# Two conditioning slices summed on VectorE, a later division, and another ring for the odd layer's conditioning tiles

## Chip, cores and metric

The kernel runs on one core of one Trainium2 chip. The metric is the device time of one execution in microseconds; lower is better. PE is TensorE, DVE VectorE, ACT ScalarE, POOL GpSimd, SP SyncE, whose queue issues most transfers.

## The reference

A two-layer diffusion backbone over 512 latent tokens (a grid of 8 rows and 64 columns, 1024 channels) and 256 context tokens. Cut to what matters here:

```python
for l in range(2):
    sh1, sc1, g1, sh2, sc2, g2 = split(silu(c) @ ada_w[l] + ada_b[l], 6)   # ada_w: (1024, 6144) per layer
    u = rmsnorm(x, norm1_g[l]) * (1 + sc1) + sh1
    y = even_mixer(u, u_ctx) if l == 0 else odd_mixer(u)
    x = x + g1 * (y @ w_out[l])
    x = x + g2 * hier_moe(rmsnorm(x, norm2_g[l]) * (1 + sc2) + sh2)

# even_mixer: q, k, v and three convolution inputs by projection; 8 heads of neighbourhood attention over
# 512 window keys and the context keys together: softmax(q k / 8 + bias) v, beside a short gated convolution
# odd_mixer: three Hyena parts (long convolutions by a DFT) beside a Conformer convolution; 20 projections
```

The 6144 conditioning columns of a layer are three slices of 2048: slice (l, 0) is sh1 and sc1, (l, 1) is g1 and sh2, (l, 2) is sc2 and g2. Only sh1 and sc1 of layer 0 are needed at the start; the others are due later.

## The kernel before

All is fp32. A large product is done as three matmuls of rounded parts (`mm3`, lines 159 to 161): `split` (lines 145 and 146) makes `whi` on ACT and `wlo` on DVE from a loaded 512 KB tile `raw`. The tiles come from rings: `raw` has 5 buffers, `whi` and `wlo` 4 each. A ring gives its oldest buffer, so a load waits on the SP queue until the last reader of that buffer is done, and everything behind it on SP waits too.

The program runs in stages: the start of the conditioning and the K projection (to about 76 us), V, Q and the twelve gated-convolution projections `proj_ch` (to about 210), the attention (to about 310), `w_out`, routing and sixteen expert blocks of layer 0 (to about 590), the odd layer with twenty projections `P(c)`, four long convolutions (`chain`) and four Conformer parts (to about 835), then `w_out` and experts again.

The conditioning slices are spread as a filler through two stages. `ada` (line 209) loads two 512 KB tiles per step and multiplies them on PE with the column `cT` (line 225; 32 output columns, four column groups side by side; 64 records per slice). `ada_sums` (line 229) adds the tiles on DVE instead, scaled by the conditioning value (lines 246 and 248), and sums over the partitions by four matmuls (line 254). Before the change `rest` (line 449) runs slices (0,1), (0,2) and (1,0) by `ada`; the odd layer runs (1,1) and (1,2) by `ada_sums`. `tick` advances the filler by `PRE[0]` per V and Q tile, `PRE[1]` per `proj_ch` and `PRE[2]` per attention step. The first slice's tiles go into the four attention-bias buffers (`self.spare`), which are free until the attention bias is loaded; the later ones into the `raw` ring. In the odd layer `ORDER` mixes the steps (`t1`) with projections, and the sums' tiles share the `raw` ring with `w_in_odd` (20 tiles) and `cfx` (4).

The attention has 16 steps (4 pairs of heads, 4 query tiles). `scores` (line 540) adds the bias and takes the row maximum on DVE (line 554), the exponential and its sum `z` on ACT (line 558). `values` (line 562) divides the probabilities by `z` on DVE (lines 565 and 566), transposes them on PE (line 569), copies them (lines 572 and 574) and multiplies by V (line 580). After four steps `ya` is split (lines 604 and 605).

Each engine runs its instructions in one fixed order. A scheduler sets it when the kernel is built, so a change in one place can move instructions elsewhere. At line 225 one step does:

```python
for g in range(4):
    nc.tensor.matmul(ps[32 * g:32 * g + 32, :], self.cT[:, k, :],
                     raws[g // 2][:, (g % 2) * 512:(g % 2) * 512 + 512], start=(k == 0), stop=(k == 7))
```

Of the kernel before, what the change touches and what calls it, by code (L numbers as in the profile page):

```python
# [8 lines left out]
F32 = mybir.dt.float32  # L9
# [3 lines left out]
AF = mybir.ActivationFunctionType  # L13
ALU = mybir.AluOpType
# [5 lines left out]
LN_EPS = 1e-5  # L20
WIN0 = (0, 64, 192, 256)
PAT = (0, 1, 1, 2)
PRE = [0.4, 0.5, 1.5]
PLO = (0, 0)
HMD = [[1, 2, 3], [0, 1, 3]]
HMA = [[], [0, 1, 2]]
# [35 lines left out]
PM = 1  # L62
PJ = 2
PU = [[], []]
ORDER = 'p1 t1 v1 t1 v0 t1 p0 t1 c0 t1 A0 t1 v3 t1 v2 t1 p2 t1 c2 t1 p3 t1 c1 t1 A1 x0 t1 c3 t1 x1 t1 B0 t1 x2 L0 x3 B1 t9'
TWO_PI = (6.28125, 0.0019350051879882812, float(2.0 * math.pi - 6.28125 - 0.0019350051879882812))
P_, Q_ = (0, 1, 2, 3), (4, 5, 6, 7)
NP1, NP2, NQ2, NQ3 = 8, 9, 10, 11
# [2 lines left out]
class Build:  # L71
# [158 lines left out]
    def ada_sums(self, l, j):  # L230

        nc, A = self.nc, self.A
        b = A["ada_b"]
        bias = self.wk.tile([128, 512], F32, tag="t2", name="adab")
        nc.gpsimd.dma_start(bias, bass.AP(tensor=b.tensor, offset=b.offset + l * 6144 + j * 2048,
                                          ap=[[512, 4], [0, 32], [1, 512]]))
        for h in range(2):
            acc = self.ep2.tile([128, 1024], F32, tag="adaacc", name="adaacc", bufs=1)
            c0 = j * 2048 + h * 1024
            for k in range(8):  # L240
                raw = self.spare.pop(0) if self.spare else self.rawp.tile([128, 1024], F32, tag="raw", name="raw")
                if self.spare:
                    self.spare.append(raw)
                nc.sync.dma_start(raw, A["ada_w"][l, k * 128:k * 128 + 128, c0:c0 + 1024])
                if k == 0:
                    nc.vector.tensor_scalar(acc, raw, self.cT[:, k, 0:1], None, op0=ALU.mult)
                else:
                    nc.vector.scalar_tensor_tensor(acc, raw, self.cT[:, k, 0:1], acc, op0=ALU.mult, op1=ALU.add)
                if k % 2:
                    yield  # L250
            if not h:
                ps = self.mmt()
            for g in (2 * h, 2 * h + 1):
                nc.tensor.matmul(ps[32 * g:32 * g + 32, :], self.onec.to_broadcast([128, 32]), acc[:, (g % 2) * 512:(g % 2) * 512 + 512],
                                 start=True, stop=True)
        self.ada_done(l, j, ps, bias)

    def ada_done(self, l, j, ps, bias):
        nc, A = self.nc, self.A
# [117 lines left out]
    def even(self, st):  # L377
        nc, A = self.nc, self.A
# [3 lines left out]
        ep2 = self.ep2 = self.pool(st, "ep2", 2)  # L382
# [11 lines left out]
        bias = [ep.tile([128, 4, 256], F32, name=f"bias{i}") for i in range(4)]  # L394
# [53 lines left out]

        def rest():
            for l, j in ((0, 1), (0, 2), (1, 0)):  # L450
                yield from self.ada(l, j)

        self.fill, self.due, self.hold = rest(), 0, None
        W = WV
# [52 lines left out]
        for s in range(4):  # L507
# [6 lines left out]
            m = ep2.tile([128, 528], F32, tag="cm", name="cm", bufs=1)  # L514
# [19 lines left out]
            if s == 2:  # L534
                qk = prep(0)
# [1 line left out]
        vblk = ((vt[:, 0, :], vt[:, 1, :]), (vs[:, 0, :], vs[:, 1, :]), (vs[:, 1, :], vs[:, 2, :]),  # L537
                (vt[:, 2, :], vt[:, 3, :]))

        def scores(qk, j):  # L540

            qs, ks, bs = qk
            pes = []
            for i in range(2):
                s = self.sct()
                for n0, k0 in ((0, WIN0[j]), (256, 512)):
                    for p in range(2):
                        nc.tensor.matmul(s[:, n0:n0 + 256], qs[:, i, p, j * 128:j * 128 + 128],
                                         ks[:, i, k0:k0 + 256], start=(p == 0), stop=(p == 1))
                pt = PAT[j]  # L550
                bsl = bs[i][:, pt:4:3 - pt, :]
                pe = ep2.tile([128, 512], F32, tag="pe", name="pe", bufs=4)
                nm = ep2.tile([128, 1], F32, tag="nm", name="nm", bufs=4)
                nc.vector.tensor_tensor_reduce(pe.rearrange("p (a b) -> p a b", a=2),
                                               s.rearrange("p (a b) -> p a b", a=2), bsl, -1.0, 3.0e38,
                                               op0=ALU.add, op1=ALU.min, accum_out=nm)
                z = ep2.tile([128, 1], F32, tag="z", name="z", bufs=4)
                nc.scalar.activation(pe, pe, AF.Exp, bias=nm, scale=-1.0, accum_out=z)
                pes.append((pe, z))
            return pes  # L560

        def values(c, j, pes, pv):
            pts = []
            for i, (pe, z) in enumerate(pes):
                nc.vector.reciprocal(z, z)
                nc.vector.tensor_scalar(pe, pe, z, None, op0=ALU.mult)
                tp = self.trt()
                for bl in range(4):
                    nc.tensor.transpose(tp[:, bl * 128:bl * 128 + 128], pe[:, bl * 128:bl * 128 + 128], self.ident)  # L569
                pT = ep2.tile([128, 4, 128], F32, tag="pT", name="pT", bufs=3)  # L570
                if i == 0:
                    nc.scalar.copy(pT.rearrange("p a b -> p (a b)"), tp)
                else:
                    nc.vector.tensor_copy(pT.rearrange("p a b -> p (a b)"), tp)
                pts.append(pT)
            for bl in range(4):
                for i in range(2):
                    h = 2 * c + i
                    v = vblk[j][bl] if bl < 2 else vt[:, 2 + bl, :]
                    nc.tensor.matmul(pv[64 * i:64 * i + 64, j * 128:j * 128 + 128], v[:, h * 64:h * 64 + 64],  # L580
                                     pts[i][:, bl, :], start=(bl == 0), stop=(bl == 3))

        ya = [self.bp.tile([128, 4, 512], F32R, tag="b8", name="ya") for _ in range(2)]
        pes = scores(qk, 0)
        for n in range(16):
            c, j = n // 4, n % 4
            if j == 0:
                pv = self.mmt()
            if j == PJ and c < 3:
                qk2 = prep(c + 1)  # L590
            if j == 3 and c < 3:
                qk = qk2
                if c < 2:
                    rel_bias(c + 2)
            nxt = scores(qk, (j + 1) % 4) if n < 15 else None
            self.tick(PRE[2])
            if n == 13:
                for _ in self.fill:
                    pass
                self.W0 = self.chunk(A["w_out"][0], 0)  # L600
            values(c, j, pes, pv)
            pes = nxt
            if j == 3:
                nc.scalar.copy(ya[0][:, c, :], pv)
                nc.vector.tensor_tensor(ya[1][:, c, :], pv, ya[0][:, c, :], op=ALU.subtract)
        self.yh = [ya[0][:, s, :] for s in range(4)] + [yc[0][:, s, :] for s in range(4)]
        self.yl = [ya[1][:, s, :] for s in range(4)] + [yc[1][:, s, :] for s in range(4)]

# [204 lines left out]
    def odd(self, st):  # L813
# [80 lines left out]
        fill = self.ada1  # L894
        for w in ORDER.split():
            if w[0] == "t":
# [631 lines left out]
```

## Time and profile before

| | |
|---|---|
| median of 3 runs | 1126.87 us (1123.34 to 1130.07) |
| the profiled execution | 1123.78 us |
| its span, first to last instruction | 1121.7 us, so 2.1 us lie around it |
| mean granted TensorE clock | 0.944 |
| busy share of the span | PE 91%, DVE 69%, ACT 44%, POOL 21% |

The profile gives busy time per engine, the chain of work that ended last, groups of instructions, and by stretch the granted TensorE clock and the share of the DMA engines. Matmuls overlap: a matmul's duration is longer than the step from one start to the next, so a stretch is read by start times.

### The profile page before, as it was taken

The page shows a single profiled execution, that of the slowest core. Times are in us where ns is not written, and L with a number is a line of the kernel's source. Part 1 is how long each engine was busy: PE and PEld are TensorE (multiplying, and loading weights), DVE is VectorE, ACT ScalarE, POOL GpSimd, SP SyncE. Part 2 cuts the span into 40 slices and gives each one's busy share as a digit, 9 for nine tenths or more (in the row PEclk, how much of TensorE's full clock was granted, in tenths as well). Part 3 has the DMA queues.
Part 4 walks back from the last instruction along what each step waited for, and adds up shares of the span by engine and source line. Part 5 has one row for each costly group of instructions (what it writes and reads, how often), then busy time and mean ns, then how long its engine had stood idle before and what let it go on. Part 6 is the DMA issues. An engine that isn't in the chain of part 4 may idle for free.

```text
span 1121.7 us, 14655 instructions
## 1 busy us (share of the span) xinstructions
PE 1023.0 (91%) x5118; PEld 755.2 (67%) x5118; DVE 774.0 (69%) x1255; ACT 497.9 (44%) x787; POOL 230.4 (21%) x244
## 2 busy tenths in 40 slices
PE   6999999999999599999987889899899859999994
PEld 2786787556787477777756667576477747777663
DVE  3462335587658798897967677757754577998883
ACT  3352223356434476577625323221253236766652
POOL 2031304011053223354221000000002121333311
PEclk8999999998999599999988899899989778999998
DMA  8825563686364479999825657634418786799893
GB/s 342 319 68 166 164 198 128 245 267 220 121 222 177 153 228 349 307 317 299 270 61 205 224 148 232 192 94 142 140 56 268 258 269 211 242 307 322 283 291 79
DMA packets 75374, 240.78 MB, mean 215 GB/s; under 512 B 15887, under 2 KB 17706, under 8 KB 75296
## 3 DMA queue, kind: packets, MB, share of 16 engines
q1 hardware_dynamic: 59840, 209.82, 55.0%
q0 software_dynamic: 15456, 29.98, 10.6%
q8 instruction: 42, 0.69, 0.3%
q14 instruction: 36, 0.29, 0.1%
HBM read 227.40 MB, written 25.72 MB: 226 GB/s over the span
## 4 chain that ended last, share of the span: by engine, by line
PE 65%; DMA 17%; DVE 8%; issue 5%; ACT 3%; POOL 1%; SPq 0%; POOLq 0%; DVEq 0%; ACTq 0%
PE mm L159 13%; PE mm L160 13%; PE mm L161 12%; DMA out<-eo,gi 6%; PE mm L225 3%; PE mm L1364 3%; PE sc L621 3%; PE mm L807 3%; DMA raw<-in_w_in_odd 2%; PE mm L580 2%; DVE wlo L146 2%; PE mm L621 2%; PE tr L1318 2%; DMA raw<-in_moe 2%; PE tr L569 2%
## 5 line engine op out<-in xcount | busy, mean ns | idle before, releaser
L146 DVE TENSOR_TENSOR wlo<-raw,whi 128x1024 fp32r<-128x1024 f32 x199 | 242.8, 1231 | 93.9 <-ACT whi L145 93.2
L145 ACT CAST whi<-raw 128x1024 fp32r<-128x1024 f32 x199 | 206.6, 1051 | 159.8 <-DMA raw<-in_w_in_odd 59.9
L159 PE MATMUL mm<-whi,xt 128*128 128x512 f32 x208 | 87.0, 418 | 2.4 <-ACT whi L145 2.4
L160 PE MATMUL mm<-wlo,xt 128*128 128x512 f32 x208 | 85.6, 412 | 3.3 <-DVE wlo L146 3.0
L161 PE MATMUL mm<-whi,xt 128*128 128x512 f32 x208 | 83.9, 403 | 0.0
L159 PE MATMUL mm<-u,whi 128*128 128x512 f32 x160 | 65.8, 414 | 5.9 <-ACT whi L145 5.3
L1307 POOL DMA_INDIRECT xe<-hd,gi x34 | 44.9, 1320 | 108.5 <-PE tr L1318 81.9
L161 PE MATMUL mm<-u,wlo 128*128 128x512 f32 x160 | 64.4, 404 | 0.3 <-DVE wlo L146 0.2
L160 PE MATMUL mm<-u,whi 128*128 128x512 f32 x160 | 64.4, 404 | 0.0
L1318 PE MATMUL tr<-ident,xe 128*128 128x128 f32 x264 | 41.6, 285 | 18.3 <-DMA xe<-hd,gi 16.0
L159 PE MATMUL mm<-whi,at 128*128 128x512 f32 x132 | 54.6, 448 | 1.0 <-ACT at L1378 0.9
L1396 DVE SCALAR_TENSOR_TENSOR eo<-mm,sw,gb 128x512 f32<-128x512 f32 x66 | 47.6, 744 | 10.6 <-PE mm L161 10.4
L160 PE MATMUL mm<-wlo,at 128*128 128x512 f32 x132 | 53.1, 417 | 0.0
L1397 POOL DMA_INDIRECT out<-eo,gi x17 | 33.2, 1953 | 96.1 <-DVE eo L1396 36.1
L1321 ACT CAST xt<-tr 128x512 fp32r<-128x512 f32 x66 | 32.4, 496 | 43.6 <-PE tr L1318 43.3
L161 PE MATMUL mm<-whi,at 128*128 128x512 f32 x132 | 51.0, 407 | 0.6 <-DVE at L1379 0.6
L1318 PEld LDWEIGHTS tr<-ident,xe 128*128 128x128 f32 x264 | 33.4, 148 | 26.3 <-issue 18.4
L160 PEld LDWEIGHTS mm<-wlo,xt 128*128 128x128 f32 x208 | 40.5, 195 | 14.7 <-DVE wlo L146 6.3
L159 PEld LDWEIGHTS mm<-whi,xt 128*128 128x128 f32 x208 | 40.3, 194 | 11.5 <-ACT whi L145 3.3
L1397 POOL DMA_INDIRECT xd<-eo,gi x16 | 33.3, 2079 | 71.7 <-DVE eo L1396 44.7
L1324 DVE TENSOR_TENSOR xt<-tr,xt 128x512 fp32r<-128x512 f32 x66 | 37.4, 570 | 14.8 <-ACT xt L1321 10.6
L743 POOL MEMSET pad<- 128x1 f32 x12 | 1.2, 100 | 225.5 <-DVE x L750 158.0
(402 smaller groups left out, 2439.0 us busy)
## 6 DMA issues: line engine op xcount, KB each, us to landing
raw<-in_moe SPq DMA_DIRECT2D x143, 512.0 KB
raw<-in_ada_w SPq DMA_DIRECT2D x64, 512.0 KB
mr<-in_moe SPq DMA_DIRECT2D x47, 512.0 KB
raw<-in_w_in_odd SPq DMA_DIRECT2D x20, 512.0 KB
bias<-in_ada_w SPq DMA_DIRECT2D x16, 512.0 KB
raw<-in_w_out SPq DMA_DIRECT2D x16, 512.0 KB
raw<-in_w_qkv SPq DMA_DIRECT2D x12, 512.0 KB
raw<-in_w_gch SPq DMA_DIRECT2D x12, 512.0 KB
```

The source lines that it names most:

```text
L145: nc.scalar.copy(hi, raw3)
L146: (lo_engine or nc.vector).tensor_tensor(lo, raw3, hi, op=ALU.subtract)
L159: nc.tensor.matmul(ps, lh, rh, start=first, stop=False)
L160: nc.tensor.matmul(ps, lh, rl, start=False, stop=False)
L161: nc.tensor.matmul(ps, ll, rh, start=False, stop=last)
L225: nc.tensor.matmul(ps[32 * g:32 * g + 32, :], self.cT[:, k, :], raws[g // 2][:, (g % 2) * 512:(g % 2) * 512 + 512], start=(k == 0), stop=( ...
L621: nc.tensor.matmul(ps[:, g * 256:g * 256 + 256], D[:, mat, :], s[:, r, :], start=(n == 0), stop=(n == 1))
L1307: self.fetched = self.nc.gpsimd.indirect_dma_start(out=xe, out_offset=None, in_=self.hd[l][:, :], in_offset=bass.IndirectOffsetOnAxis(ap=g ...
L1318: nc.tensor.transpose(pt[:, k * 128:k * 128 + 128], xe[:, (4 * h + k) * 128:(4 * h + k) * 128 + 128], self.ident)
L1324: nc.vector.tensor_tensor(xt[:, 1, 4 * h:4 * h + n, :].rearrange("p a b -> p (a b)"), pt[:, 0:n * 128], hi, op=ALU.subtract)
L1396: nc.vector.scalar_tensor_tensor(o[:, sl], ps, wt, g2b[:, sl], op0=ALU.mult, op1=ALU.mult)
L1397: nc.gpsimd.indirect_dma_start(out=self.dst[l][:, :], out_offset=bass.IndirectOffsetOnAxis(ap=di, axis=0), in_=o, in_offset=None, bounds_c ...
```

## The change

Slices (0,1) and (0,2) go to `ada_sums`, with all tiles in the four attention-bias buffers; the `PRE` values are such that both are through before those buffers are needed. Slice (1,0) stays with `ada`. `ada_sums` loads the bias row last and has two more stops per slice. The division by `z` moves behind the product with V: the eight sums of four steps stand in one tile, one reciprocal is taken, eight small matmuls spread the reciprocals over a PSUM tile laid out as the output, ACT copies it, DVE multiplies. In the odd layer the sums' tiles come alternately from the `whi` and `wlo` rings of `split`; `ORDER` has other places for the steps.

```diff
-PRE = [0.4, 0.5, 1.5]
+PRE = [1.1, 1.1, 0.6]
...
-ORDER = 'p1 t1 v1 t1 v0 t1 p0 t1 c0 t1 A0 t1 v3 t1 v2 t1 p2 t1 c2 t1 p3 t1 c1 t1 A1 x0 t1 c3 t1 x1 t1 B0 t1 x2 L0 x3 B1 t9'
+ORDER = 'p1 t1 v1 t1 v0 t1 p0 t1 c0 t2 A0 v3 t1 v2 t1 p2 t1 c2 t2 p3 t1 c1 t2 A1 x0 t1 c3 t2 x1 t1 B0 x2 L0 x3 B1 t9'
...
-                raw = self.spare.pop(0) if self.spare else self.rawp.tile([128, 1024], F32, tag="raw", name="raw")
-                if self.spare:
+                if l and j:
+                    raw = self.wp.tile([128, 1024], F32, tag=("whi", "wlo")[k % 2], name="adaw")
+                else:
+                    raw = self.spare.pop(0)
                     self.spare.append(raw)
...
-                yield from self.ada(l, j)
+                yield from self.ada_sums(l, j) if l == 0 else self.ada(l, j)
...
-                nc.scalar.activation(pe, pe, AF.Exp, bias=nm, scale=-1.0, accum_out=z)
+                nc.scalar.activation(pe, pe, AF.Exp, bias=nm, scale=-1.0, accum_out=zs[:, 2 * j + i:2 * j + i + 1])
...
-                nc.vector.reciprocal(z, z)
-                nc.vector.tensor_scalar(pe, pe, z, None, op0=ALU.mult)
...
-                nc.scalar.copy(ya[0][:, c, :], pv)
-                nc.vector.tensor_tensor(ya[1][:, c, :], pv, ya[0][:, c, :], op=ALU.subtract)
+                nc.vector.reciprocal(zs, zs)
+                zb = self.mmt()
+                for m in range(8):
+                    i, q = m % 2, slice(m // 2 * 128, m // 2 * 128 + 128)
+                    nc.tensor.matmul(zb[64 * i:64 * i + 64, q], zs[:, m:m + 1].to_broadcast([128, 64]), self.ident,
+                                     start=True, stop=True)
+                y = self.wk.tile([128, 512], F32, tag="t2", name="ya")
+                nc.scalar.copy(y, zb)
+                nc.vector.tensor_tensor(y, pv, y, op=ALU.mult)
+                nc.scalar.copy(ya[0][:, c, :], y)
+                nc.vector.tensor_tensor(ya[1][:, c, :], y, ya[0][:, c, :], op=ALU.subtract)
```

The change moves instructions. On DVE at the end of the K projection (about 53 to 58 us before), where `u` and `ul` are the last two of eight latent input tiles and `uc` the first of the context, before:

```order
L297 SCALAR_TENSOR_TENSOR adac_101<-adac_101,adc 128x4
L354 TENSOR_SCALAR u_464<-tr,adac_101 128x512
L354 TENSOR_SCALAR u_473<-tr,adac_101 128x512
L355 TENSOR_TENSOR ul<-u_464,ul 128x512
L355 TENSOR_TENSOR ul<-u_473,ul 128x512
L354 TENSOR_SCALAR u_504<-tr,adac_101 128x256
L354 TENSOR_SCALAR u_511<-tr,adac_101 128x256
L355 TENSOR_TENSOR uc<-u_504,uc 128x256
```

and on DVE in the same place now (line numbers of the changed file, five higher here):

```order
L302 SCALAR_TENSOR_TENSOR adac_101<-adac_101,adc 128x4
L245 TENSOR_SCALAR adaacc<-bias_122,cT 128x1024
L359 TENSOR_SCALAR u_464<-tr,adac_101 128x512
L247 SCALAR_TENSOR_TENSOR adaacc<-bias_123,cT,adaacc 128x1024
L359 TENSOR_SCALAR u_473<-tr,adac_101 128x512
L360 TENSOR_TENSOR ul<-u_464,ul 128x512
L247 SCALAR_TENSOR_TENSOR adaacc<-bias_124,cT,adaacc 128x1024
L360 TENSOR_TENSOR ul<-u_473,ul 128x512
L359 TENSOR_SCALAR u_504<-tr,adac_101 128x256
L359 TENSOR_SCALAR u_511<-tr,adac_101 128x256
L247 SCALAR_TENSOR_TENSOR adaacc<-bias_125,cT,adaacc 128x1024
L360 TENSOR_TENSOR uc<-u_504,uc 128x256
```

Four of the new sums stand between the tiles that the K projection waits for; four more stand among the next six `uc` tiles.

On SP at the start of the odd layer (about 587 us before), after the four loads of `xd`, before:

```order
L1106 DMA xr_5439<-xd 128x1024
L136 DMA raw<-in_w_in_odd 128x1024
L244 DMA raw<-in_ada_w 128x1024 x2
L136 DMA raw<-in_w_in_odd 128x1024
L244 DMA raw<-in_ada_w 128x1024 x2
L136 DMA raw<-in_w_in_odd 128x1024
```

and on SP in the same place now:

```order
L1121 DMA xr_5364<-xd 128x1024
L136 DMA raw<-in_w_in_odd 128x1024 x5
L243 DMA adaw<-in_ada_w 128x1024 x4
L136 DMA raw<-in_w_in_odd 128x1024
L136 DMA raw<-in_cfx 128x1024
L243 DMA adaw<-in_ada_w 128x1024
L136 DMA raw<-in_w_in_odd 128x1024
```

Five projection tiles now go out ahead of the first conditioning tile, where one stood ahead of two.

## Rows read from the trace of the kernel before

**Rows 1.** Page, busy time over the span; then the chain's shares by engine.

```profile
PE 1023.0 (91%) x5118; PEld 755.2 (67%) x5118; DVE 774.0 (69%) x1255; ACT 497.9 (44%) x787; POOL 230.4 (21%) x244
PE 65%; DMA 17%; DVE 8%; issue 5%; ACT 3%; POOL 1%; SPq 0%; POOLq 0%; DVEq 0%; ACTq 0%
```

**Rows 2.** Stretches: length, busy PE, PEld, DVE, ACT, POOL (instructions), clock, DMA share, GB/s.

```profile
46.00:76.00 30.00, 29.87 (x151) 24.37 (x146) 17.93 (x35) 13.32 (x23) 2.92 (x3) 1.00 0.41 149
76.00:137.00 61.00, 61.00 (x276) 43.50 (x274) 21.91 (x33) 17.21 (x23) 18.07 (x16) 1.00 0.49 152
137.00:205.00 68.00, 68.00 (x317) 52.49 (x318) 27.50 (x36) 19.61 (x28) 14.00 (x26) 1.00 0.58 185
...
222.00:262.00 40.00, 40.00 (x297) 22.08 (x295) 29.43 (x72) 22.07 (x45) 8.46 (x8) 1.00 0.85 278
262.00:310.00 48.00, 45.27 (x338) 37.00 (x334) 35.54 (x88) 25.71 (x55) 2.35 (x4) 0.89 0.45 146
...
616.00:700.00 84.00, 75.44 (x368) 56.60 (x366) 63.47 (x69) 25.99 (x35) 2.42 (x16) 0.96 0.66 203
700.00:790.00 90.00, 83.70 (x432) 55.55 (x432) 63.96 (x71) 20.11 (x28) 0.26 (x4) 0.96 0.49 147
```

**Rows 3.** Groups to 400 us: line, engine, form, count, busy us, mean ns, idle before.

```profile
L225 PE MATMUL mm<-raw,cT 128*32 128x512 f32 x128 | 25.8, 603 | 1.0 <-DMA raw<-in_ada_w 1.0
L225 PE MATMUL mm<-bias,cT 128*32 128x512 f32 x64 | 11.0, 603 | 0.0
```

**Rows 4.** PE in order of time: start, length, line, form [idle before, released by].

```profile
108.41 1.90 PE L225 MATMUL mm<-bias,cT 128*32 128x512 f32 x10
110.25 0.74 PE L159 MATMUL mm<-whi,ul 128*128 128x512 f32 x2
...
237.86 1.09 PE L580 MATMUL mm<-pT,vt 128*64 128x128 f32 x14
```

**Rows 5.** Odd layer: PE's four `ada_sums` records (chain); DVE's sums, min/median/max ns.

```profile
770.25 1.01 PE mm L254 x4
...
L248 DVE SCALAR_TENSOR_TENSOR adaacc<-raw,cT,adaacc x28: 1260/1279/1286, 615.1 to 784.5; 128x1024 f32<-128x1024 f32 x28
```

**Rows 6.** Groups to 400 us: the division, and the split of the output.

```profile
L566 DVE TENSOR_SCALAR pe<-pe,z 128x512 f32<-128x512 f32 x32 | 16.2, 510 | 0.3
...
L565 DVE RECIPROCAL z<-z 128x1 f32<-128x1 f32 x32 | 4.9, 157 | 2.4 <-ACT pe L558 2.3
...
L605 DVE TENSOR_TENSOR ya<-mm,ya 128x512 fp32r<-128x512 f32 x4 | 2.8, 688 | 2.1 <-ACT ya L604 2.1
```

**Rows 7.** DVE in order of time, end of the K projection.

```profile
52.93 0.16 DVE L297 SCALAR_TENSOR_TENSOR adac<-adac,adc 128x4 f32<-128x4 f32 x1
54.00 1.53 DVE L354 TENSOR_SCALAR u<-tr,adac 128x512 f32<-128x512 f32 x2 [0.91 <-ACT ul L351]
55.45 1.28 DVE L355 TENSOR_TENSOR ul<-u,ul 128x512 fp32r<-128x512 f32 x2
```

**Rows 8.** PE in order of time, attention, third pair of heads.

```profile
263.63 1.09 PE L580 MATMUL mm<-pT,vt 128*64 128x128 f32 x14
264.65 1.21 PE L548 MATMUL sc<-ks,qs 128*128 128x256 f32 x8
267.16 0.66 PE L569 MATMUL tr<-ident,pe 128*128 128x128 f32 x4 [1.30 <-DVE pe L566]
...
277.09 1.97 PE L580 MATMUL mm<-pT,vt 128*64 128x128 f32 x14
```

**Rows 9.** PE in order of time, the odd layer's three long gaps.

```profile
626.51 0.79 PE L159 MATMUL mm<-u,whi 128*128 128x512 f32 x1 [4.99 <-ACT whi L145]
...
704.80 1.12 PE L760 MATMUL tr<-ident,x 128*128 128x128 f32 x4 [5.19 <-ACT ur L761]
...
792.03 7.00 PE L621 MATMUL sc<-ur,D 128*128 128x256 f32 x24 [3.22 <-ACT b L624]
```

**Rows 10.** Waits from 640 to 880 us: who, for whom, total us, times, longest.

```profile
ACT whi L145 <- DMA raw<-in_w_in_odd: 44.8, 10, 10.0
...
DVE adaacc L248 <- DMA raw<-in_ada_w: 5.3, 5, 3.4
```

**Rows 11.** Chain, odd layer, three waits for a tile: start and length.

```profile
616.43 8.96 DMA raw<-in_w_in_odd
...
679.59 4.43 DMA raw<-in_w_in_odd
...
695.06 8.13 DMA raw<-in_w_in_odd
```

More of the change, by code (lines that the diff above doesn't have):

```diff
@@ L233, in ada_sums @@
         b = A["ada_b"]
-        bias = self.wk.tile([128, 512], F32, tag="t2", name="adab")
-        nc.gpsimd.dma_start(bias, bass.AP(tensor=b.tensor, offset=b.offset + l * 6144 + j * 2048,
-                                          ap=[[512, 4], [0, 32], [1, 512]]))
         for h in range(2):
@@ L255, in ada_sums @@
                                  start=True, stop=True)
+            if not h:
+                yield
+        bias = self.wk.tile([128, 512], F32, tag="t2", name="adab")
+        nc.gpsimd.dma_start(bias, bass.AP(tensor=b.tensor, offset=b.offset + l * 6144 + j * 2048,
+                                          ap=[[512, 4], [0, 32], [1, 512]]))
         self.ada_done(l, j, ps, bias)
+        yield
     def ada_done(self, l, j, ps, bias):
@@ L538, in even, with scores @@
                 (vt[:, 2, :], vt[:, 3, :]))
-        def scores(qk, j):
+        def scores(qk, j, zs):
             qs, ks, bs = qk
@@ L556, in scores @@
                                                op0=ALU.add, op1=ALU.min, accum_out=nm)
-                z = ep2.tile([128, 1], F32, tag="z", name="z", bufs=4)
-                nc.scalar.activation(pe, pe, AF.Exp, bias=nm, scale=-1.0, accum_out=z)
-                pes.append((pe, z))
+                nc.scalar.activation(pe, pe, AF.Exp, bias=nm, scale=-1.0, accum_out=zs[:, 2 * j + i:2 * j + i + 1])
+                pes.append(pe)
             return pes
@@ L563, in values @@
             pts = []
-            for i, (pe, z) in enumerate(pes):
-                nc.vector.reciprocal(z, z)
-                nc.vector.tensor_scalar(pe, pe, z, None, op0=ALU.mult)
+            for i, pe in enumerate(pes):
                 tp = self.trt()
@@ L583, in even @@
         ya = [self.bp.tile([128, 4, 512], F32R, tag="b8", name="ya") for _ in range(2)]
-        pes = scores(qk, 0)
+        zsum = lambda: ep2.tile([128, 8], F32, tag="z", name="z", bufs=2)
+        zs = zsum()
+        pes = scores(qk, 0, zs)
         for n in range(16):
@@ L594, in even @@
                     rel_bias(c + 2)
-            nxt = scores(qk, (j + 1) % 4) if n < 15 else None
+            zn = zsum() if j == 3 else zs
+            nxt = scores(qk, (j + 1) % 4, zn) if n < 15 else None
             self.tick(PRE[2])
@@ L603, in even @@
             if j == 3:
-                nc.scalar.copy(ya[0][:, c, :], pv)
-                nc.vector.tensor_tensor(ya[1][:, c, :], pv, ya[0][:, c, :], op=ALU.subtract)
+                nc.vector.reciprocal(zs, zs)
[9 more added lines that the diff above has]
+                nc.vector.tensor_tensor(ya[1][:, c, :], y, ya[0][:, c, :], op=ALU.subtract)
+                zs = zn
         self.yh = [ya[0][:, s, :] for s in range(4)] + [yc[0][:, s, :] for s in range(4)]
```

## The prediction

> **What bounds the kernel now.** I read the page first: PE is busy for 91% of the span and stands for 65% of the chain, DMA for 17%, DVE for 8% [rows 1]. Then the stretches [rows 2]. From 46 to 262 us PE is busy all the time at full clock, while DVE works 17.93 of 30, 21.91 of 61 and 27.50 of 68 us and the DMA engines are half idle: in the projections a microsecond of PE work is a microsecond of time, and DVE has room. From 262 to 310 us PE is still busy for 45.27 of 48, but the granted clock is 0.89 and DVE works 35.54 of 48: the attention's second half is set by both. The odd layer is the third place: PE idles 8.6 of 84 and 6.3 of 90 us, at a clock of 0.96, with the DMA engines at 0.66 and 0.49. The waits say why: ACT's split waited 44.8 us for `w_in_odd` tiles, DVE's sums only 5.3 us for theirs [rows 10]. The projection tiles come late, not because DMA is full but because the ring of five is shared.
>
> **The change part by part: matmuls taken from PE.** Three slices cost PE 11.0 + 25.8 = 36.8 us [rows 3]; (0,1) is the 11.0, (0,2) half of 25.8, so 23.9. The length of a group reaches beyond the next start: the group at 108.41 lasts 1.90 and the next matmul starts after 1.84 [rows 4], so some 0.07 us overlap in each of about 27 groups. I take 22; the ends are 21 and 23.9. Each slice keeps four matmuls in two groups. One such group of four records takes 1.01 us in the odd layer [rows 5], so two slices give back 4 us. Net 18 less. PE stands in a stretch where it never waits, so this is on the path, unless the matmuls filled time in which PE would have waited (a rival below).
>
> **The sums on DVE.** 32 tiles at 1.28 us [rows 5] are 41 us. From 46 to 205 us DVE is free for 12.1 + 39.1 + 40.5 = 91.7 us [rows 2], so most of it lies beside PE's work. It does not at the end of the K projection. There DVE is on PE's path: it waits 0.91 us for ACT and then makes `u` and `ul` without a pause [rows 7]. Four sums now stand in that run, the first of which fits into the 0.91 us; the other three put the last `ul` and the first `uc` later by up to 3.8 us, and four more among the next `uc` tiles add up to 5.1 us, against 12.1 us of idle time in 46 to 76. PE has other matmuls (the halves that need only `whi` and the tiles done earlier), so not all of it is seen. Bounds 0 and 8.9 us, nearest the four sums that delay `ul`: I take +3.
>
> **The division.** DVE loses 16.2 + 4.9 us and gets four products of 0.69 us like line 605 and four reciprocals: 21.1 less, 3.4 more [rows 6]. ACT gets four more copies, PE four sets of eight matmuls with 64 output columns. The nearest row is line 580's group with 64 columns too, 1.09 us for 14 records [rows 4]; sixteen records would be 1.2, so 4 x 1.1 to 1.3; I take +4.4 on PE, which is the path as long as PE is full. Behind the last pair of heads the product puts 0.7 us more ahead of `w_out`, hidden by matmuls on the convolution half. What DVE gives back shows where PE waited for it: PE waited 1.30 us for line 566 at 267, and afterwards the same work ran at nearly half speed, 1.97 us at 277 against 1.09 at 263 [rows 8]. A clock of 0.89 over 48 us is 5.3 us, and the idle time 2.7. The division leaves that chain, but the `w_out` splits that crowd DVE there stay, and the fillers that PE has up to 262 become fewer: of the 8 us I take 3 back (bounds 8 back, and 10 more lost).
>
> So the even layer gives -22 + 4 + 4.4 + 3 - 3 = -13.6 us.
>
> **The odd layer.** Five `w_in_odd` tiles now go out ahead of the sums' tiles, so the first six projections do not wait for the shared ring, and a later tile waits on SP only where it stands behind a sum's tile whose buffer is not free. Two gaps of PE end with ACT held by a late `w_in_odd` tile: 4.99 us before 626.51 and 5.19 us before 704.80 [rows 9]; the tiles landed 8.96 and 8.13 us after their issue, at 625.4 and 703.2 [rows 11]. That is 10.2 us. The clock of 0.96 over 84 and 90 us costs 3.4 + 3.6 = 7.0 us more [rows 2], nearly all behind these gaps. The third gap, 3.22 us before 792.03, has ACT waiting for a `w_out` tile, which still stands among sums' tiles on SP; I leave it. Against 17.2 us stand the new waits: of four buffers each of `whi` and `wlo`, a projection now finds only about two, and a split that follows a sum's tile in the ring waits for the transfer and for DVE; the transfers took 4.4 to 9.0 us [rows 11]. A projection is 24 matmuls of 0.22 us (61 us over 276 records in the second stretch [rows 2]), 5.3 us, so a wait shows only beyond that. I take four such waits of 2 us. Net -9 (bounds -20, all three gaps and the clock, and +2).
>
> Sum: 1123.78 - 13.6 - 9 = 1101.2 us. That is against the profiled execution; the median of the runs shown is 3.1 us above it and the fastest 0.4 below, and I do not correct for it.
>
> **The rivals.** *The odd layer gives nothing.* The sums' tiles take the split ring's buffers as they took the raw ring's before; a split then waits for issue, transfer and sum, some 9.0 + 1.3 us, of which a projection of 5.3 us hides half. Four such waits are 19 us and eat the 17.2. For it: only two buffers per projection are left. Against it: the raw tiles themselves are now all loaded ahead. Time 1123.8 - 13.6 = 1110.
>
> *The attention loses its clock.* Slice (0,2)'s matmuls were PE's filler at the attention's start, and the attention now has one step of `ada` for each 1.7 steps where it had 1.5 for each. PE then waits for DVE or ACT in each step, as at 267 [rows 8], and runs at the lower of its two clock levels (1.2 instead of 2.4 GHz) for about 39 us, where the 5.3 us lost by the clock of 0.89 are 10.6 us at that level: 14 us more. Time 1101 + 14 = 1115. Against it: DVE has 17.7 us less to do there. The Trainium skill ("TensorE: Matmul & The Clock Gate", "HAM oscillation — how this bites in real kernels") describes this: bursts of matmuls that alternate with waits start cold each time and run at half clock for a while. By that rule the trace agrees, since the half-speed stretch stands right behind the wait at 267.
>
> *The sums jam the projections: slower.* DVE runs in order, so a sum that waits for its tile holds the splits behind it. The 32 tiles go through four buffers: eight rounds, each a landing plus 4 x 1.28 us. With the longest landing seen, 9.0 us, that is 8 x 14.1 = 113 us; between 53 us, where the first sum stands [rows 7], and the loading of the bias, nine projections of 5.3 us after Q's end at 137, there are 132. So it decides from a landing of 11.4 us on, and each further microsecond costs 8: at 14.2 the whole gain is gone, at 15.1 the time is 1131. Against it: the DMA share there is 0.49 and 0.58 [rows 2], with 16 tiles more to move in that time.
>
> *PE does not get shorter.* The conditioning matmuls filled seams between projections, where the next split is not ready, and PE waits there instead. For it: at 108.41 ten records stand between V's last matmul and Q's first [rows 4]. Against it: no idle time stands around them [rows 3]. Then 22 us are not saved: 1123.
>
> **How the numbers follow.** The forecast 1101 has 0.50, the odd layer without gain (1110) 0.20, the lost clock (1115) 0.12, the seams (1123) 0.08, the jam (1131) 0.10. The low end is the forecast with most of the odd layer's 20 us and the attention's 8: 1123.8 - 13.6 - 5 - 20 = 1085, rounded down to 1084 for the 23.9. The high end takes in the lost clock and stops short of the seams and the jam: 1121. A measurement can tell about 0.5% from no change, 5.6 us. Faster by more than that: the first two cases and nine tenths of the third, less the forecast's own tail, 0.79. Within it: the seams and the rest, 0.11. Slower: the jam, 0.10.
>
> **What would show it.** In the changed profile: no line 225 before the attention's slice (1,0), and the first attention step some 10 us earlier; lines 565 and 566 gone, and DVE under 60% in the attention; no gap of 5 us on PE at the second projection of the odd layer, and ACT's wait for `w_in_odd` under 15 us. Wrong it is if PE waits over 6 us in all for DVE between 50 and 80 us, if PE waits for DVE behind a sum that waits for its tile, if ACT's split waits for sums in the odd layer by over 15 us, or if the clock in the attention stays under 0.9.

## The result, and the profile after

The changed kernel took 1112.1 us (median of 4 runs, 1111.64 to 1115.19) beside 1126.4 us of the kernel before in the same comparison: a ratio of 0.9883 with a 95% interval of 0.9846 to 0.9921. Measured again beside the experiments it came to 0.9901 (0.9867 to 0.9935). By the ratios it is faster by 11 to 13 us, as forecast in sign, but by about half of the forecast 22.6 us (the medians of the first comparison differ by 14.3). The profiled execution took 1111.64 us, its span is 1109.8.

The page of after, busy time and chain, to be read beside [rows 1]:

```profile
PE 1007.9 (91%) x5070; PEld 752.6 (68%) x5070; DVE 800.3 (72%) x1231; ACT 500.0 (45%) x791; POOL 240.7 (22%) x244
PE 23%; DMA 11%; DVE 5%; issue 5%; ACT 2%; SPq 1%; POOL 0%; POOLq 0%; DVEq 0%; ACTq 0%
```

PE has 15 us less to do and DVE 26 us more. The chain of after can be followed back through less than half of the span (its shares add up to 47%), so its shares are not compared with those before. The stretches of after with the borders of [rows 2] (length, busy time of PE, PEld, DVE, ACT, POOL, then clock, DMA share, GB/s):

```profile
46.00:76.00 30.00, 29.13 (x139) 23.11 (x139) 22.87 (x37) 12.85 (x22) 0.00 (x0) 1.00 0.80 264
76.00:137.00 61.00, 61.00 (x268) 48.63 (x268) 37.46 (x49) 18.45 (x26) 20.97 (x15) 1.00 0.56 182
137.00:205.00 68.00, 64.23 (x289) 48.34 (x287) 48.80 (x54) 19.23 (x28) 15.18 (x25) 0.97 0.70 216
222.00:262.00 40.00, 33.47 (x266) 26.37 (x266) 29.67 (x56) 26.89 (x52) 8.91 (x9) 0.87 0.50 168
262.00:310.00 48.00, 48.00 (x384) 39.62 (x381) 25.63 (x55) 24.46 (x52) 8.73 (x16) 0.96 0.45 153
616.00:700.00 84.00, 79.60 (x389) 59.05 (x390) 62.97 (x68) 29.22 (x40) 1.67 (x15) 0.98 0.60 190
700.00:790.00 90.00, 85.85 (x440) 55.68 (x439) 67.76 (x77) 18.84 (x27) 0.26 (x4) 0.98 0.54 164
```

Before, PE never waited in these stretches from 76 to 205 and from 222 to 262 us (between them, which the prediction did not read, it lacked 1.0 us of 17). Now it lacks 3.8 us between 137 and 205 and 6.5 us between 222 and 262, at a clock of 0.87. In return 262 to 310 is full at 0.96 where it lacked 2.7 at 0.89: the attention's weak place has moved forward. The odd layer is fuller and its clock is 0.98 for 0.96.

The stages, from each kernel's profile. The borders are PE's first attention score, the end of its last product with V, and its first row of the expert blocks of layer 0 (the first gathered tile), of the odd layer (the first odd projection) and of the odd layer's norm. "Behind it" is the stretch from the attention's end to the expert blocks, which holds `w_out` and the routing.

| kernel | first score at | attention | behind it | expert blocks at | expert blocks 0 | odd layer | norm to end |
|---|---|---|---|---|---|---|---|
| before | 194.6 | 115.2 | 68.2 | 378.1 | 221.8 | 228.5 | 293.2 |
| sums alone | 193.9 | 111.8 | 68.1 | 373.7 | 224.6 | 230.8 | 290.5 |
| division alone | 195.1 | 114.4 | 74.9 | 384.4 | 220.3 | 232.9 | 297.9 |
| sums and division | 193.6 | 105.2 | 72.2 | 370.9 | 220.3 | 234.4 | 290.7 |
| odd part alone | 194.0 | 115.4 | 68.0 | 377.4 | 219.1 | 220.0 | 295.7 |
| after | 194.1 | 105.6 | 72.6 | 372.4 | 224.2 | 221.9 | 291.4 |
| after, again | 191.0 | 101.4 | 73.3 | 365.8 | 226.1 | 223.0 | 295.4 |

In after's profile the even layer gained 5.7 us up to the expert blocks, of which 2.4 were lost in them, and the odd layer 6.6. One kernel's stages differ by up to 7 us between two profiles (the two lines of after), so a stage is judged by several kernels below.

**Where the even layer lost it.** First the bias row. These rows are POOL's, DVE's and PE's, each in order of time (start, length, line, form, idle time before and its releaser):

```profile
130.49 1.45 POOL L258 DMA_DIRECT2D adab<-in_ada_b  x2
...
134.82 1.21 DVE L146 TENSOR_TENSOR wlo<-raw,whi 128x1024 fp32r<-128x1024 f32 x1
144.59 0.69 DVE L266 TENSOR_TENSOR adar<-mm,adab 128x512 f32<-128x512 f32 x1 [8.55 <-DMA adab<-in_ada_b]
...
146.46 1.22 DVE L146 TENSOR_TENSOR wlo<-raw,whi 128x1024 fp32r<-128x1024 f32 x1
...
141.26 0.39 PE L161 MATMUL mm<-ul,wlo 128*128 128x512 f32 x1
145.42 0.47 PE L159 MATMUL mm<-ul,whi 128*128 128x512 f32 x1 [3.77 <-DVE adar L266]
...
145.96 0.53 PE L161 MATMUL mm<-ul,wlo 128*128 128x512 f32 x1
146.28 0.63 PE L159 MATMUL mm<-ul,whi 128*128 128x512 f32 x1
```

The row that the change loads last was issued at 130.5, and the addition that reads it began 14.1 us later. PE waited 3.77 us for the end of this addition and then ran at 0.63 us a matmul where it had 0.39. It did not wait for weights: its first matmul needs only `whi`, and its first with `wlo` runs at 145.96, before the next split on DVE starts (146.46). The addition reads the PSUM tile in which PE has summed the slice, one of four `mm` tiles (`PB`), so PE most likely waited for that buffer; no run separates this.

Second the attention. DVE, then PE, in order of time:

```profile
233.33 1.83 DVE L146 TENSOR_TENSOR wlo<-raw,whi 128x1024 fp32r<-128x1024 f32 x1
235.19 0.42 DVE L503 CAST qs<-qs 64x512 fp32r<-64x512 f32 x1
235.64 1.23 DVE L146 TENSOR_TENSOR wlo<-raw,whi 128x1024 fp32r<-128x1024 f32 x1
236.90 0.76 DVE L500 SCALAR_TENSOR_TENSOR qs<-mm,gq,qs 64x512 fp32r<-64x512 f32 x1
237.69 0.69 DVE L559 CUSTOM_DVE_ANT_1 pe<-sc,bias 128x512 f32<-128x512 f32 x1
...
238.44 0.80 PE L553 MATMUL sc<-ks,qs 128*128 128x256 f32 x2 [2.04 <-DVE nm L559]
```

PE waits for a row maximum that stands behind two splits of `w_out`. There are four of these, at 226 to 237 us; before they stood at 265 to 273, where [rows 8] shows the wait and the half-speed group. They follow the end of slice (1,0), which frees the `raw` ring; that slice now ends at 226 us instead of 262.7, because it starts during the last projections.

Third the stretch behind the attention, which nobody edited: 72.6 us for 68.2. Three rows of ACT and one of PE after, then two of ACT and one of PE at the same place before, each in order of time:

```profile
344.43 1.28 ACT L677 ACT_TABLE_LOAD   x1
345.85 1.71 ACT L677 ACTIVATE seq<-delta,tcol 128x256 f32<-128x256 f32 x4
347.46 0.56 ACT L1025 COPY xT<-tr 128x512 f32<-128x512 f32 x1
348.07 1.07 PE L1031 MATMUL sc<-wa,xT 128*128 128x20 f32 x8 [1.89 <-ACT xT L1025]
...
351.95 0.57 ACT L1010 COPY xT<-tr 128x512 f32<-128x512 f32 x1
352.54 1.28 ACT L662 ACT_TABLE_LOAD   x1
353.89 0.97 PE L1016 MATMUL sc<-wa,xT 128*128 128x20 f32 x8
```

Before, the copy `xT` for the router stands on ACT ahead of a table load (1.28 us); now it stands behind the load and four more passes, and PE waits 1.89 us for it. The scheduler has set another order. Of the fourteen profiles here, the eight with this order take 71.9 to 76.3 us for the stretch and the six with the old one 68.0 to 69.8. All eight have the late division, but so have three of the six, so the division comes with the new order in some kernels and not in others. No run changes the order alone.

**Where the odd layer won.** ACT's waits there, from 590 to 860 us (total, times, longest), beside [rows 10]:

```profile
ACT whi L145 <- DVE adaacc L247: 27.6, 4, 11.9
...
ACT whi L145 <- DMA adaw<-in_ada_w: 5.5, 1, 5.5
```

Two of PE's longest gaps there, in order of time, beside [rows 9]:

```profile
616.67 0.50 PE L161 MATMUL mm<-u,wlo 128*128 128x512 f32 x1 [2.13 <-DVE wlo L146]
...
781.05 1.92 PE L253 MATMUL mm<-adaacc,onec 128*32 128x512 f32 x4 [3.18 <-DVE adaacc L247]
```

The wait for `w_in_odd` tiles is gone, and with it the gaps of 4.99 and 5.19 us. ACT now waits for sums instead, 27.6 us, and PE hardly feels it.

### The profile page after: what moved, and what is told of

It is laid out like the page before. It is cut to its first block, busy times and chain, and to the rows that moved or that the text cites. A ratio compares the mean times of both kernels' runs of the same rounds, so it can differ in the third digit from the quotient of the medians.

```text
span 1109.8 us, 14573 instructions
## 1 busy us (share of the span) xinstructions
PE 1007.9 (91%) x5070; PEld 752.6 (68%) x5070; DVE 800.3 (72%) x1231; ACT 500.0 (45%) x791; POOL 240.7 (22%) x244
## 5 line engine op out<-in xcount | busy, mean ns | idle before, releaser
L1411 DVE SCALAR_TENSOR_TENSOR eo<-mm,sw,gb 128x512 f32<-128x512 f32 x66 | 47.6, 744 | 12.9 <-PE mm L161 12.7
L1333 PEld LDWEIGHTS tr<-ident,xe 128*128 128x128 f32 x264 | 33.4, 147 | 22.6 <-issue 15.0
L1412 POOL DMA_INDIRECT xd<-eo,gi x16 | 31.4, 1963 | 74.0 <-DVE eo L1411 21.3
L1339 DVE TENSOR_TENSOR xt<-tr,xt 128x512 fp32r<-128x512 f32 x66 | 37.4, 570 | 12.7 <-ACT xt L1336 7.9
```

The source lines that it names most:

```text
L1333: nc.tensor.transpose(pt[:, k * 128:k * 128 + 128], xe[:, (4 * h + k) * 128:(4 * h + k) * 128 + 128], self.ident)
L1339: nc.vector.tensor_tensor(xt[:, 1, 4 * h:4 * h + n, :].rearrange("p a b -> p (a b)"), pt[:, 0:n * 128], hi, op=ALU.subtract)
L1411: nc.vector.scalar_tensor_tensor(o[:, sl], ps, wt, g2b[:, sl], op0=ALU.mult, op1=ALU.mult)
L1412: nc.gpsimd.indirect_dma_start(out=self.dst[l][:, :], out_offset=bass.IndirectOffsetOnAxis(ap=di, axis=0), in_=o, in_offset=None, bounds_c ...
```

## The experiments

Medians are device microseconds; a ratio is to the kernel before on the same chip, with its 95% interval. "After" is 1112.

### Each part alone

**Sums alone**: the kernel before with these edits and the even slices' new generator.

```diff
-PRE = [0.4, 0.5, 1.5]
+PRE = [1.1, 1.1, 0.6]
...
-                yield from self.ada(l, j)
+                yield from self.ada_sums(l, j) if l == 0 else self.ada(l, j)
```

> Before, with the two even slices on DVE and the new PRE alone; division, split ring and ORDER of the odd layer as before. The prediction's own terms (22 us of matmuls gone, 4 for the sums, 3 at the K projection, nothing lost in the attention) give 1126.4 - 15 = 1111. The theory that the late bias row costs PE a wait and a cold clock (3.8 + 2.0 us, read from the trace of after at 145 us) gives 1117. The theory that also the attention pays for its lost filler (about 4 us more of idle time and slow matmuls) gives 1121.

Measured: 1124.5 us, ratio 0.9988 (0.996 to 1.0016): no gain. The attention of this kernel, as a stretch:

```profile
222.00:262.00 40.00, 31.38 (x226) 24.30 (x224) 35.81 (x76) 25.00 (x48) 8.33 (x8) 0.90 0.44 162
```

Two rows of PE in it, then two of DVE, each in order of time:

```profile
236.87 0.73 PE L602 MATMUL tr<-ident,pe 128*128 128x128 f32 x4 [1.58 <-DVE pe L599]
255.28 0.63 PE L602 MATMUL tr<-ident,pe 128*128 128x128 f32 x4 [1.66 <-DVE pe L599]
...
233.36 2.97 DVE L146 TENSOR_TENSOR wlo<-raw,whi 128x1024 fp32r<-128x1024 f32 x2
236.25 0.47 DVE L599 TENSOR_SCALAR pe<-pe,z 128x512 f32<-128x512 f32 x1
```

PE is busy for 31.4 of 40 us where it had 40.0 [rows 2], and DVE for 35.8 where it had 29.4. Without the conditioning matmuls PE waits for DVE, here for the division (line 599), which stands behind two splits. The third theory comes nearest: much of the filler's time comes back as waiting.

**Division alone**, the attention's part of the diff on the kernel before.

> Before, with the late division alone. By the prediction's terms, +4.4 us on PE and 3 us back from DVE: 1127 to 1128. The theory that the attention was held by DVE while it had its filler gives up to 8 us back: 1122 to 1123. The theory that DVE never held PE there gives only the added matmuls: 1130 to 1131.

Measured: 1132.5 us, ratio 1.006 (1.0032 to 1.0087): slower. The same stretch:

```profile
222.00:262.00 40.00, 40.00 (x295) 21.84 (x293) 24.02 (x47) 21.27 (x42) 10.36 (x11) 1.00 0.80 254
```

The spreading matmuls of this kernel as a group of 190 to 320 us (count, then busy us and mean ns):

```profile
L608 PE MATMUL mm<-ident,z 128*64 128x128 f32 x64 | 5.1, 281 | 0.0
```

The attention's second half, beside 45.27 at 0.89 before [rows 2]:

```profile
262.00:310.00 48.00, 48.00 (x380) 36.78 (x379) 30.33 (x63) 27.64 (x57) 2.13 (x4) 0.93 0.55 186
```

The number is that of the third theory or a little above it, but the mechanism is not. DVE did hold PE there in spite of the filler: the 2.7 us of idle time are gone and the clock is 0.93, so 3.4 us are lost from 222 to 310 where 8.0 were, and with the added matmuls the attention is as long as before (114.4 us for 115.2). The loss stands behind the attention: 74.9 us for 68.2, in the new order.

**Sums and division together**, after with the odd layer's old tiles and order.

> After without its odd part: sums and division in the even layer, the odd layer's tiles and order as before. If the parts add up, 1125.2 - 0.7 + 7.3 = 1132. The theory that the division pays only where the sums have taken PE's filler (with the sums alone PE waits 10.5 us between 194 and 262 us, partly for the division, with both 7.1) gives what after has above the odd layer alone: 1125.2 - 13 + 11.3 = 1123 to 1124.

Measured: 1118.7 us, ratio 0.9947 (0.9921 to 0.9973). The two parts, which alone give -0.7 and +7.3 us, give -5.8 together. Sums take PE's filler away and make DVE late; the division takes DVE's lateness away at a price on PE. Neither pays by itself. The time is below both expectations: that the parts work together was right, by how much was not. In the profiles the division shortens the attention by 6.6 us where the filler is gone (105.2 for 111.8) and by 0.8 where it is there, and lengthens the stretch behind by 4.1 and 6.7.

**Odd part alone**, `ORDER` and the split ring's tiles on the kernel before, with the new generator's late bias row and two more stops.

> Before, with the odd layer's tiles in the split ring and its ORDER alone. The prediction's term is -9 us: 1117. The trace of after shows the odd layer, from its first projection to the norm, 6.6 us shorter (228.5 to 221.9): 1120. The rival that the split's waits for sums (27.6 us on ACT in the trace of after) cost as much as they bring gives 1125 to 1127.

Measured: 1113.9 us, ratio 0.9892 (0.9857 to 0.9927), 11 to 12 us: a gain as large as that of the whole change. The same wait as in after, from 590 to 860 us:

```profile
ACT whi L145 <- DVE adaacc L247: 28.9, 4, 11.7
```

What stands in its place in sums and division together, which has the old odd layer:

```profile
ACT whi L145 <- DMA raw<-in_w_in_odd: 58.3, 14, 10.5
```

The rival that waits for sums eat the gain is out: 28.9 us of them on ACT, and the kernel is 11 us faster. Over all profiles the odd layer takes 228.5 to 234.4 us with the old tiles (mean 231.7 of four) and 219.9 to 225.9 with the new (mean 221.8 of ten): 9.9 us less. Whether the ring or the order brings it, no run separates.

**After, again**, beside these.

> The changed kernel again, beside the others on the same chip: 1112, and by the parts measured alone (sums -0.7, division +7.3, odd layer -11.3) 1120.5 if they add up.

Measured: 1112.0 us, ratio 0.9901 (0.9867 to 0.9935). Sums and division (-5.8) and the odd part (-11.3) would add to 1107.5; the intervals of the parts reach 1112, and whether some 4 us are lost between them is open.

### The bias row

**All rows of the sums early**: the row goes straight into the result's tile once the first half is summed.

```diff
             if not h:
                 ps = self.mmt()
+                bias = self.ep2.tile([128, 512], F32, tag="adar", name="adar", bufs=1)
+                nc.gpsimd.dma_start(bias, ...)
...
-        bias = self.wk.tile([128, 512], F32, tag="t2", name="adab")
-        nc.gpsimd.dma_start(bias, ...)
```

> After, with the bias row of the DVE sums loaded when the first half of a slice is summed, straight into the tile of the result (no other tile changes). The theory that DVE's wait of 8.55 us for this row, with the splits queued behind it, cost PE 3.77 us and a cold clock of 2.0 us, and that nothing else is late there, gives 1112.1 - 5.5 = 1106.5, and no gap of PE over 1 us between 137 and 165 us. The rival that the next sum's tile, or the split behind it, is late anyway in this DMA-heavy stretch gives 1110 to 1112 and a gap of PE in the same place, held by another wait.

Measured: 1110.4 us, ratio 0.9847 (0.9805 to 0.9889). The stretch from 130 to 160 us, this kernel and after:

```profile
130.00:160.00 30.00, 30.00 (x133) 23.92 (x132) 24.85 (x27) 9.24 (x12) 7.00 (x8) 1.00 0.97 301
```

```profile
130.00:160.00 30.00, 26.23 (x108) 20.31 (x107) 20.23 (x25) 8.16 (x11) 6.42 (x10) 0.94 0.94 271
```

The gap is gone, 133 matmuls stand where 108 stood, and the expert blocks start at 368.2 for 372.4. The end does not show it beyond doubt: the median is only 1.6 us below after, where the rival put it, the ratio is 0.9847 for 0.9901, and the intervals overlap. But no other wait stands in the gap's place, which the rival needs. In the odd layer one tile for all rows made POOL wait 19.4 us, so the next run leaves that layer as it was.

**The even layer's rows alone early** (the same edit under `if l == 0`).

> After, with the early bias row in the even layer alone; the odd layer's bias rows stay where after has them, since with all of them early POOL waited up to 19 us for the single tile there. The bias theory expects what the profile with all rows early showed for the even layer, its expert blocks reached 4.2 us earlier than in after's first profile, at the end as well: 1107 to 1108. The rival that the expert blocks of layer 0 take back what comes early expects 1110 to 1112.

Measured: 1107.0 us, ratio 0.9831 (0.9793 to 0.987), 5 us below after (the two intervals touch), expert blocks at 364.4. That is the size that the theory asks for, and with no gap left it shows the late row as the cause of the gap, whatever PE waited for behind it. The stretch is full here too, at a clock of 1.00. In five other profiles of kernels with the late row DVE waited 7.1 to 8.6 us for it and PE 2.3 to 3.8.

### The attention's filler

**Slice (1,0) held for the attention.**

```diff
+                if j == 2:
+                    for _ in range(8):
+                        yield
```

> After, with eight empty steps of the filler ahead of slice (1,0), so that its 64 matmuls start in the middle of the attention and no longer during the last projections. The theory that the attention pays for the lost filler (after: 7.1 us idle and 6.6 us of slow matmuls between 194 and 262 us, before: 2.0 and 1.6) gives about half of the 10 us back: 1107, with the long waits of PE for DVE at 235 to 246 us gone. The rival that a step of the attention is held by its chain over PE, DVE and ACT wherever PE has nothing else gives the same idle time earlier, between 194 and 235 us, and 1111 to 1113.

Measured: 1116.7 us, ratio 0.9941 (0.9918 to 0.9964): 4.6 us slower than after. Its two stretches:

```profile
222.00:262.00 40.00, 40.00 (x337) 26.01 (x336) 25.68 (x58) 26.24 (x56) 6.25 (x7) 1.00 0.55 200
262.00:310.00 48.00, 41.12 (x281) 31.57 (x280) 20.18 (x37) 17.08 (x32) 5.66 (x10) 0.89 0.59 201
```

That is slower than either expectation. PE is full from 222 to 262 as before and lacks 6.9 us after it: the weak place moved back to where it was before the change. The four splits of `w_out` moved too, to 269 to 283 us. So the place of the filler is not the cause by itself; the splits behind it go along. The attention takes 111.7 us for 105.6, the stretch behind it 68.8, in the old order.

**The early rows (all) and the held slice.**

> The early bias row and the held filler together. If both theories hold, 5.5 and 5 us less than after: 1102. If only the bias row matters, 1107 to 1110, as the bias row alone. If the stretches behind the attention give the gain back, the first expert block of layer 0 starts 10 us earlier than in after (372.4) and the end still comes at 1110.

Measured: 1114.6 us, ratio 0.9899 (0.9859 to 0.9939), above all three expectations. The first attention score came 5 us earlier than in after (189.0 for 194.1), and the held slice gave that back in the attention (116.4 us for 105.6).

**The splits of `w_out` late**, where `marks` holds the exponentials of all steps, two a step.

```diff
-                self.W0 = self.chunk(A["w_out"][0], 0)
+                with self.tc.issue_after(marks[17].ins):
+                    self.W0 = self.chunk(A["w_out"][0], 0)
```

> After, with the four loads and splits of w_out in the attention held until the exponential of the ninth step. In after they stand on DVE at 226 to 237 us, as soon as slice (1,0) frees the raw ring, among the rows for the second pair of heads, and PE waits 1.12 and 2.04 us behind them and then runs part of 240 to 262 us at a granted clock of 0.81. The theory that these splits are what the attention lost to expects 4 to 6 us less, 1106 to 1108, and no wait over 1 us of PE for DVE between 228 and 250 us. The rival that the steps are held by their own chain wherever PE has no filler expects the waits to stay and 1111 to 1113; a worse case is that w_out's matmuls, which now fill the attention's end, come late: 1115.

Measured: 1107.2 us, ratio 0.9835 (0.9801 to 0.9868). The stretch, beside 33.47 at 0.87 in after:

```profile
222.00:262.00 40.00, 35.90 (x319) 30.14 (x317) 31.84 (x62) 29.30 (x57) 7.20 (x6) 0.96 0.35 107
```

319 matmuls stand where 266 stood, and no wait of PE for DVE exceeds 1 us up to 250. The splits were at 251 to 258. The time is as expected, 5 us below after, and the intervals touch. This supports the crowd on DVE, but the profiles say it less firmly: the attention takes 101.2 us here and 102.4 with both edits, and 101.4 to 107.6 in the five profiles with sums, late division, early splits and a free filler, the lowest of them after, again. In this one profile the bias row happened to land at 139.8, without a gap on PE, so the profile's early expert blocks (363.0) are not all its merit.

**Both edits.**

> Both edits together. If both theories hold, 1112 - 4.5 - 5 = 1102 to 1103; if only one of them, 1107; if the expert blocks take it back, 1110.

Measured: 1106.2 us, ratio 0.9819 (0.978 to 0.9858): the best kernel here, 6 us below after, but less than the sum of the two gains, which would be 1102. The interval's low end is 1102 too, so that they do not add is not shown. In its profile the attention begins as early as with the early row (187.8) and is nearly as short as with the late splits (102.4 us); the stretch behind it is the longest of all, 76.3 us for 71.9 and 74.1, and the expert blocks begin at 366.6.

### The price of the spreading

```diff
-                for m in range(8):
+                for m in [*range(8), *range(8)]:
```

> After, with the eight matmuls that spread the reciprocals run twice in each of the four places: it doubles the division's cost on PE, priced at 4 x 1.1 us. If that cost lies on the path in after, 1112 + 4.4 = 1116.5, and it is part of the missing gain. If PE's waits in the attention hide it, 1112, and the 7.3 us that the division cost by itself came from somewhere else than these matmuls.

Measured: 1115.9 us, ratio 0.9913 (0.9883 to 0.9943), about 4 us above after, with intervals that overlap. The group in this kernel, and in after:

```profile
L613 PE MATMUL mm<-ident,z 128*64 128x128 f32 x128 | 11.8, 310 | 0.0
```

```profile
L613 PE MATMUL mm<-ident,z 128*64 128x128 f32 x64 | 5.5, 317 | 0.0
```

6.3 us more of busy time and 4 more on the end by the medians, but 1.4 by the ratios. And the edit brought the old order back behind the attention (69.8 us for 72.6), while the attention took 109.2 for 105.6. So the two expectations are not told apart, and how much of the spreading lies on the path stays open.

## Why the prediction was right, and where it was not

The sign, the mechanism of the odd layer and the range held; the even layer's sum did not. That 1112 lies in the range owes something to luck: the range is 37 us wide, the odd layer gave more than forecast where the even layer gave less, and the number that came nearest is a rival's (1110, the odd layer without gain), whose mechanism the odd part alone refutes. By parts: forecast -13.6 for the even layer, measured -5.8 (its interval is about 3 us each way); forecast -9 for the odd layer, measured -11 to -12 alone, and -9.9 over all profiles.

**Matmuls removed: nearly right in size.** Groups of after to 400 us, beside [rows 3]:

```profile
L225 PE MATMUL mm<-raw,cT 128*32 128x512 f32 x64 | 11.5, 601 | 0.0
...
L253 PE MATMUL mm<-adaacc,onec 128*32 128x512 f32 x16 | 4.2, 604 | 0.0
```

36.8 less 11.5 is 25.3 us of busy time, beside the 23.9 from which the prediction took 2 off for overlap; the sums' matmuls are 4.2, for 4. Their place was wrong: of the 36.8 us only the 11.0 of slice (0,1) stood ahead of the first score before, the 25.8 of [rows 3] behind it. So no more than some 7 us could come ahead of the attention, not the 10 of the prediction's first sign.

**Sums at the K projection: 3 us was too much.** From 46 to 76 us PE lacks 0.9 us where it lacked 0.1, and its longest gap is 0.52: the sign of error for this place, over 6 us, did not come. The other matmuls, whose inputs were ready, covered the rest.

**Division: 5.5 for 4.4 us in matmuls, and a cost behind the attention that the sum did not have.** The prediction put 0.7 us more ahead of `w_out` and held them for hidden. In after the stretch behind the attention is 4.4 us longer, and in division alone 6.7, nearly all that it lost. The held slice, with the late division and the old order, shows 0.6 of that, so most seems to come from the order.

**A cost that the prediction did not have: the bias row.** The diff said that it is loaded last, and no step priced that. In after it is 3.77 us of waiting and a clock of 0.94 over 130 to 160, some 1.8 us more: 5.6 us, of which the run with the even layer's rows early gave back 5. The sign of error "PE waits for DVE behind a sum that waits for its tile" was the right form with the wrong tile here; in the odd layer it came true by the letter (3.18 us).

**Attention jam: -3 forecast, about +5.6 in after's profile.** Before, 222 to 310 us lost 2.7 us of idle time and 5.3 by the clock [rows 2]; after, 6.5 idle and 5.2 by the clock in the first stretch and 1.9 in the second. Division alone gave 4.6 back, so DVE's relief was priced well for a PE that keeps its fillers. The step that failed took the `w_out` splits as staying where they were. They follow the end of slice (1,0), and moved with it onto the rows for the second pair of heads. The sign of error on the clock came true in that stretch, 0.87 from 222 to 262; over the whole attention the clock is 0.93. This is the rival of the lost clock in part, and the held slice shows that more filler there is not the cure. The Trainium skill ("TensorE: Matmul & The Clock Gate", "HAM oscillation — how this bites in real kernels") says that bursts of matmuls between waits start cold again; the trace agrees, at 146 us behind the wait of 3.77 (0.63 for 0.39 us a matmul).

By place, after's even layer is -0.5 us up to the first score, where the bias row took nearly all of the gain, -9.6 in the attention, where 14.3 us of the filler were taken out, and +4.4 behind it: -5.7 in that profile. Over the three profiles with this even layer it is -8.0 (372.4, 365.8 and 370.9, against 377.75, the mean of the two with the old one).

**The odd layer: right, with one test that was wrong.** Both long gaps went, as said, and near the third (3.22 us) there is now one of 3.18, behind a sum that waits for its tile. The prediction read the third as held by a `w_out` tile alone and left it out; ACT had waited for a `w_in_odd` tile just before (in order of time, before):

```profile
785.52 1.05 ACT L145 CAST whi<-raw 128x1024 fp32r<-128x1024 f32 x1 [7.99 <-DMA raw<-in_w_in_odd]
...
789.32 1.04 ACT L145 CAST whi<-raw 128x1024 fp32r<-128x1024 f32 x1 [1.42 <-DMA raw<-in_w_out]
```

I had called ACT's waits for sums of over 15 us a sign of error; they were 27.6 and cost nearly nothing. A wait of ACT counts only where PE has run out of weights, and here the split that waits is for a later projection.

**What would show it, the rest.** Line 225 is left with the 64 records of slice (1,0). The first attention score came 0.5 us earlier in after's profile (194.1 for 194.6), not 10: that was the first sign that the even layer had not paid. DVE in the attention is at 63% (65.8 us of 194 to 299), not under 60; it was 69% (79.7 us of 194 to 310).

**Open.** Layer 0's expert blocks take 220.4 us on average in the three profiles without the even sums and 222.2 in the eleven with them; norm to end is 293.1 in four with the old odd layer and 294.9 in ten with the new. So some 2 us may be given back behind each gain; no run here tells why. One candidate can be looked at. The odd layer's bias row is late too, and in after DVE's wait for it is on the chain, where before another load stood (after, then before):

```profile
835.75 12.29 DMA adab<-in_ada_b
...
845.04 12.12 DMA gainr<-in_norm_g
```

But with all rows early the norm to the end still takes 295.9 us, so this is not shown to be the reason. Open too is what the order behind the attention costs by itself.

## What to carry to other kernels

Of work that is moved, follow every load that it issues to the engine that waits for it: a 256 KB row that landed late held one addition on DVE, and PE waited for that addition. Matmuls that fill a stage bound by waits do not give their whole time back when they are removed, and a relief of the engine that PE waits for is worth more once the filler is gone: measure such parts alone and together. Then compare the stages that nobody edited: an edit can give them another order, and a time that fits a theory can come from there. A wait of an engine off the critical path is not evidence; look for the gap that it leaves on PE.

## What the hardware showed

The 256 KB bias row was issued on POOL's queue while the DMA engines were at 0.94 (130 to 160 us). The addition that waited for it began 14.1 us after the issue in after, 12.7 in after, again, and 13.0 in spread twice. That is longer than any of the 512 KB tiles of [rows 11], which were loaded at a DMA share of 0.66. The Trainium skill ("DMA: Bandwidth & Descriptors", "Rules for kernel authors") says that an outermost dimension below 16 confines a transfer to at most that many DMA engines, and this row's source has one of 4; no run here tells engines apart, so whether that is why it was slow is not shown.

Eight matmuls that spread the reciprocals leave 16 records of 0.3 us, so the four places took 4.6 to 5.5 us of PE's busy time.
